# A two-layer attention and retention trunk on one core: three dense banks instead of two, logits and probabilities in one buffer, rows turned and outputs stored in one transfer

## The chip, the cores and the metric

The kernel runs on one core of one Trainium2 chip. The metric is the device time of one execution, in microseconds. A core has five engines with instruction streams of their own: PE (TensorE: matmuls, with weight loads shown apart as PEld), DVE (VectorE), ACT (ScalarE), POOL (GpSimd) and SP (SyncE, which here issues every DMA). They meet by semaphores only.

## The reference, cut

```
for layer in range(2):
    h    = rms_norm(x, norm_gain[layer])                     # x: 2048 x 1024, f32
    proj = h @ w_in[layer]                                   # 1024 x 4096, in 8 sections of 512:
    aq, ak, av, ag, rq, rk, rv, rg = split(proj)             # attention q,k,v,gate; retention q,k,v,gate
    # attention: 8 heads x 64; a query sees its own 64-token chunk and the 8 chunks before it
    s    = aq @ ak.T * 64**-0.5 + rel_bias[head, clip(distance)]
    ya   = softmax(s) @ av
    # retention: 4 heads x 128; rotary q and k, decay per head, running state, rms norm of each head's output
    yr   = rms_norm(decayed(rq, rk) @ rv + rq @ state)
    y    = concat[ya * silu(ag), yr * silu(rg)]
    x    = x + y @ w_out[layer]                              # 1024 x 1024
out = rms_norm(x, final_gain)
```

## The kernel before

**Precision.** Every large product is done as three f16 products of high and low parts (high x high, low x high, high x low): a matrix is kept as a pair of f16 tiles, whose sum carries the f32 value. So the products of 1024 inputs take 3 x 8 = 24 matmuls for one result bank.

**Tiling.** The 2048 tokens are four blocks n of 512, each of four tiles a of 128. The input projection of a layer goes by section s = 0 to 3: two attention heads and one retention head with all their parts. For each (layer, s, n) there are two dense generators. `dense_T` makes q, k, rotary q and rotary k (j = 0 to 3) transposed, channels on partitions and the block's 512 tokens as columns, with 24 matmuls of 128x512 each (L731; L712 for the very first block, which is done tile by tile). `dense_V` makes v, retention v and both gates, one token tile at a time (L752). Both need the block's normed input transposed, `hTh` and `hTl` (high and low). Their results lie in PSUM banks of the pool `psD`, two of them; ACT and DVE read a bank out, ending with L770 for the gate tile `gt`, before the bank is used again.

**Attention** runs one block behind, as 8 units (a, hx) of one token tile and one head. A unit: PE makes the logits S (L800, L801); DVE adds the bias and takes the row maximum (L804, out: f32 buffer `sc`); DVE turns the maximum into the exponential's bias, m * nc + LN_PSC (L806); ACT takes the exponential with scale g.c (L807) and copies it to f16 (L809, buffer `pq`); POOL subtracts for the low part (L810, same `pq`); SP transposes `pq` into `pT` by DMA (L812); two units later PE multiplies with v into a bank of `psR` (L820 to L822, tile `o`, whose column 64 holds the sum of the row), and DVE divides and applies the gate (`out_`, L826 to L832), then SP stores y (L835). `sc` and `pq` have two buffers each.

**Retention** (`decayed`, `retention`) makes r1, the decayed scores of a tile, r2, its output with the carried state, and a new state; DVE makes the f16 low parts (`rest_of`, L868), POOL the power for the norm (L921), DVE applies norm and gate (L925) and SP stores its half of y.

**Rows.** Where normed rows are made on ACT and DVE, they are a pair of f16 rows, one in a buffer of `sc` and one in a buffer of `pq` (`row_pair`), and `transpose_rows` turns both with one DMA transpose each (L236, L237). That happens for the norms of the first layer's blocks 2 and 3 (during s = 0), for some norms between the layers, and for each tile's y ahead of the output projection (`y_squares` L958, `rows_hi`, `rows_lo`, `y_turn`).

**Output projection** (`wout`): 16 tiles of 48 matmuls (L1105), in six rounds a tile. `wout_first` prepares the first two y rows. The last attention units of a layer run beside its first tiles.

**Order.** The programs of PE, ACT, DVE and POOL are in the order in which the Python code emits them. Generators are advanced in rounds: `run` steps a dense generator and the attention generator together, `later(k, fn)` puts a step k rounds on, `push` queues background work (weights, norms, tables) and `pull` takes steps of it. SP's order is left to a scheduler after the first section. A wait of one instruction holds all that follow on its engine.

**The start.** Weights, the gains, rotary tables (`tables`, stored to DRAM and loaded by block) and the norms of the first eight tiles are made in the first 80 us, in an order written by hand.

Of the kernel before, what the change touches and what calls it, by code (L numbers as in the profile page):

```python
# [27 lines left out]
def hybrid_trunk(ctx: ExitStack, tc: tile.TileContext, x, pos, gain, gcol, w_in, w_out, rel, fgain,  # L28
# [33 lines left out]
    pool.memset(mhalf, -0.5)  # L62
    invf_sb = cp.tile([P, 1], F32, tag="invf", name="invf_sb")
# [6 lines left out]
    tab_d = [dp.tile([2, P, 512], F32, tag=f"tab{n}", name=f"tab{n}") for n in range(NS)]  # L70
# [12 lines left out]
    def tables(n, wk):  # L83

        ang, k, r, k2 = wk
# [40 lines left out]
        for hf in range(2):  # L126
            sl = slice(hf * 64, hf * 64 + 64)
            cs = slice(hf * 256, hf * 256 + 256)
            sp.dma_start(tab_d[n][0, 0:64, cs], k2[sl, :])
            sp.dma_start(tab_d[n][0, 64:128, cs], k2[sl, :])  # L130
            sp.dma_start(tab_d[n][1, 0:64, cs], ang[sl, :])
            sp.dma_start(tab_d[n][1, 64:128, cs], r[sl, :])
# [82 lines left out]
    def hT_of(l, n):  # L215
        if (l, n) not in hT:
            hT[l, n] = (hp.tile([P, KT, 512], F16, tag="hTh", name=f"hTh{l}_{n}"),
                        hp.tile([P, KT, 512], F16, tag="hTl", name=f"hTl{l}_{n}"))
        return hT[l, n]

    def row_pair(nm):
        return (b2.tile([P, 1280], F16, tag="sc", name=f"rh{nm}")[:, 0:D],
                b2.tile([P, 1280], F16, tag="pq", name=f"rl{nm}")[:, 0:D])
# [11 lines left out]
    def transpose_rows(rows, dh, dl):  # L235
        sp.dma_start_transpose(out=dh, in_=rows[0])  # L236
        sp.dma_start_transpose(out=dl, in_=rows[1])  # L237

    class Tok:


        def __init__(self, t, xt, rows):
            self.t, self.x, self.rows, self.nm = t, xt, rows, f"n0_{t}"
            self.hh, self.hl = (h_[:, :, t % 4 * P:(t % 4 + 1) * P] for h_ in hT_of(0, t // 4))
# [21 lines left out]
        def hi(self):  # L266
            if self.rows:
                self.rw = (self.rows[:, 0:D], self.rows[:, D:2 * D])
                act.activation(self.rw[0], self.x, AF.Copy)
                return  # L270
            for h in range(2):
                act.activation(self.hh[:, h * KT // 2:(h + 1) * KT // 2, :], self.pt[h], AF.Copy)

        def lo(self):
            if self.rows:
                dve.tensor_tensor(self.rw[1], self.x, self.rw[0], op=ALU.subtract)
                return
# [4 lines left out]
        def dma(self):  # L282
            transpose_rows(self.rw, self.hh, self.hl)
# [324 lines left out]
    def dense_T(l, s, n, g, st):  # L608
        hh, hl = hT[l, n]
        nm = f"{l}_{s}_{n}"  # L610
        st.tabc = b1.tile([P, 512], F32, tag="tabc", name=f"tabc{nm}")
        st.tabs = b1.tile([P, 512], F32, tag="tabs", name=f"tabs{nm}")
        def tab_load():
            while n not in tab_done:
                pull(1)
            sp.dma_start(st.tabc, tab_d[n][0])
            sp.dma_start(st.tabs, tab_d[n][1])
# [9 lines left out]
        def evacuate(j, ps):  # L627
            if j == 0:
                st.q = b2.tile([P, 2, 2, 512], F16, tag="q", name=f"q{nm}")
                qq = b1.tile([P, 2, 512], F16, tag="qq", name=f"qq{nm}")  # L630
# [10 lines left out]
            elif j == 1:  # L641
                st.k = b3.tile([P, 2, 512], F16, tag="k", name=f"k{nm}")
                kk = b1.tile([P, 2, 512], F16, tag="swp", name=f"kk{nm}")
                kh, kl = kk[:, 0, :], kk[:, 1, :]
                act.activation(kh, ps, AF.Copy, scale=2.0 ** -16)

                def k_rest():
                    dve.scalar_tensor_tensor(out=kl, in0=ps, scalar=2.0 ** -16, in1=kh, op0=ALU.mult, op1=ALU.subtract)
                    sp.dma_start(st.k[0:64, 0, :], kh[0:64, :])
                    sp.dma_start(st.k[64:128, 1, :], kh[64:128, :])  # L650
                    sp.dma_start(st.k[64:128, 0, :], kl[0:64, :])
                    sp.dma_start(st.k[0:64, 1, :], kl[64:128, :])

                soon(k_rest)
            else:
                w = 5 - j
                rot = b2.tile([P, w, 512], F16, tag=f"rot{j}", name=f"rot{nm}_{j}")
                if j == 2:
                    raw = rot[:, 1:3].rearrange("p a c -> p (a c)").bitcast(F32)
                else:  # L660
                    raw = b1.tile([P, 512], F32, tag="qq", name=f"raw{nm}")
                act.activation(raw, ps, AF.Copy, scale=2.0 ** -16)

                def swap(rot=rot, raw=raw, j=j):
                    swp = b1.tile([P, 512], F32, tag="swp", name=f"swp{nm}_{j}")
# [20 lines left out]
                    later(d, turned(raw, raw, st.tabc, ALU.mult))  # L686
                    later(d + 1, turned(swp, swp, st.tabs, ALU.mult))
# [30 lines left out]
        for j in range(2 if first else 0, 4):  # L718
# [19 lines left out]
    def dense_V(l, s, n, g, st):  # L738
        hh, hl = hT[l, n]
# [38 lines left out]
    def attention(l, s, n, g, st, prev, nxt):  # L778
# [4 lines left out]
        ya = {}  # L783

        def qk(a, hx):
# [10 lines left out]
            for j0, j1 in zip(cuts, cuts[1:]):  # L796
# [5 lines left out]
            v = b2.tile([P, 640], F32, tag="sc", name=f"sc{u.nm}")[:, 0:w]  # L802
            m = b2.tile([P, 1], F32, tag="mq", name=f"mq{u.nm}")
            dve.tensor_tensor_reduce(out=v, in0=S[:, 0:w], in1=g.bias[hx][:, 640 - w:640], scale=1.0, scalar=-3.0e38,  # L804
                                     op0=ALU.add, op1=ALU.max, accum_out=m)
            dve.tensor_scalar(m, m, g.nc[:, 0:1], LN_PSC, op0=ALU.mult, op1=ALU.add)  # L806
            act.activation(v, v, AF.Exp, bias=m[:, 0:1], scale=g.c[:, 0:1])  # L807
            pq = b2.tile([P, 1280], F16, tag="pq", name=f"pq{u.nm}")
# [6 lines left out]
        def pv(u):  # L815
            t = 4 * n + u.a
            o = psR.tile([P, 512], F32, tag="small", name=f"o{u.nm}")
            for b, (q_, a_) in enumerate(u.kts):
# [3 lines left out]
                pe.matmul(o[:, 0:65], u.p[:, u.nb + b, :], v_[:, 0:65], start=False, stop=(b == u.nb - 1))  # L822

            def out_():
# [14 lines left out]
        ret = retention(l, s, n, g, st)  # L839
# [30 lines left out]
    def decayed(l, s, n, g, st, a):  # L870
        nm = f"{l}_{s}_{4 * n + a}"
        cs = slice(a * P, (a + 1) * P)
        r1 = psR.tile([P, 512], F32, tag="small", name=f"r1{nm}")
        products(r1[:, 0:P], [(st.rk[:, i, cs], st.rq[:, j, cs]) for i, j in ((0, 0), (0, 1), (1, 0))])

        def upper():
            st.dT = b1.tile([P, 2, P], F16, tag="dT", name=f"dT{nm}")
            upper_of(st.dT, r1[:, P:2 * P])

        later(1, lambda: dve.tensor_tensor(r1[:, P:2 * P], r1[:, 0:P], g.msk, op=ALU.mult))  # L880
        later(2, upper)
        later(3, lambda: rest_of(st.dT, r1[:, P:2 * P]))

    def retention(l, s, n, g, st):
        for a in range(4):
# [5 lines left out]
            r2 = psR.tile([P, 512], F32, tag="small", name=f"r2{nm}")  # L891
# [6 lines left out]
            if not last:  # L898
# [16 lines left out]
                later(3, lambda sh=sh, ns=ns: rest_of(sh, ns))  # L915
# [7 lines left out]
            def fin(t=t, a=a, r2=r2, ss=ss, nm=nm):  # L923
                y = b1.tile([P, P], F32, tag="yr", name=f"yr{nm}")
# [591 lines left out]
```

## Time and profile before

| | before |
|---|---|
| median of 3 runs (lowest to highest), us | 2094.98 (2092.48 to 2095.95) |
| profiled execution, us | 2094.75 |
| its span, us | 2092.8 |
| mean granted TensorE clock | 0.991 |
| PE / DVE / ACT / POOL busy, us | 2004.4 / 1343.8 / 1141.3 / 432.9 |
| matmuls | 14014 |
| DMA, mean over the span | 150 GB/s |

The span runs from the first to the last instruction of the profiled execution. A row of the timeline has the start in us, the duration, the engine, the line, the operation with out<-in, and in square brackets the idle time of the engine before it with what ended it. A row of the view of waits has the total in us, the number of times and the longest. A row of busy time by stage has PE, PEld, DVE, ACT and POOL with their counts, then the granted clock, the share of DMA and GB/s. A 512-column matmul is shown as 0.38 us long, but the next starts 0.216 us after it, as matmuls overlap.

### The profile page before, as it was taken

What the parts mean: (1) busy time and instruction counts of PE and PEld (TensorE: products, weight loads), DVE (VectorE), ACT (ScalarE), POOL (GpSimd) and SP (SyncE); (2) the same over time, 40 slices, a digit from 0 to 9 for tenths busy, and PEclk for the clock granted to TensorE, in tenths of its full rate; (3) what the DMA queues carried; (4) which work ended last, traced back from release to release, by engine and by line L of the source; (5) the groups of instructions that cost most, each with busy time, mean ns of one, the idle gap of its engine ahead of it and who ended that gap; (6) DMA issues with size and microseconds to landing.
All of it is one profiled execution on the core that took longest, in us unless ns stands there. A gap on an engine that the chain in (4) does not pass through costs nothing.

```text
span 2092.8 us, 39599 instructions
## 1 busy us (share of the span) xinstructions
PE 2004.4 (96%) x14014; PEld 1049.4 (50%) x14014; DVE 1343.8 (64%) x4031; ACT 1141.3 (55%) x2522; POOL 432.9 (21%) x509
## 2 busy tenths in 40 slices
PE   6888999999999999998999999999999999998998
PEld 4344455555555555444444555555555555554443
DVE  7676666666656666576654666666666667656643
ACT  7455665556565654455444546554655565455432
POOL 1022222222122212121000222222222222222100
PEclk9999999999999999999999999999999999999999
DMA  8767674557476764599965556655655776558874
GB/s 247 171 127 162 136 166 114 115 112 159 110 169 133 161 166 99 113 211 260 219 185 113 120 102 142 130 121 106 155 123 118 178 156 162 117 100 183 212 199 123
DMA packets 645702, 313.65 MB, mean 150 GB/s; under 512 B 459232, under 2 KB 602080, under 8 KB 645504
## 3 DMA queue, kind: packets, MB, share of 16 engines
q1 hardware_dynamic: 645504, 311.12, 66.4%
q8 instruction: 110, 1.80, 0.4%
q14 instruction: 88, 0.72, 0.1%
HBM read 123.26 MB, written 41.98 MB: 79 GB/s over the span
## 4 chain that ended last, share of the span: by engine, by line
PE 55%; DMA 7%; DVE 5%; ACT 3%; issue 1%; SPq 1%; POOL 0%; POOLq 0%; DVEq 0%; ACTq 0%
PE dT L731 18%; PE dV L752 15%; PE dO L1105 12%; DMA pT<-pq 2%; PE r L860 2%; PE S L801 2%; PE S L800 2%; PE o L820 1%; PE o L821 1%; PE o L822 1%; DVE sc L804 1%; DMA swp<-rot 1%; DMA yhy<-rhy 1%; ACT sc L807 1%; ACT pq L809 1%
## 5 line engine op out<-in xcount | busy, mean ns | idle before, releaser
L810 POOL TENSOR_TENSOR pq<-sc,pq 128x640 f16<-128x640 f32 (+4 forms) x256 | 323.8, 1265 | 1175.9 <-issue 590.7
L807 ACT ACTIVATE sc<-sc,mq,cT 128x640 f32<-128x640 f32 (+4 forms) x256 | 218.5, 853 | 558.1 <-DVE mq L806 413.7
L752 PE MATMUL dV<-whV,hTh 128*128 128x512 f16 x1024 | 354.5, 382 | 13.0 <-DVE gt L770 12.8
L731 PE MATMUL dT<-hTh,whT 128*128 128x512 f16 x1008 | 349.4, 382 | 14.7 <-DMA hTh<-hTl 9.6
L752 PE MATMUL dV<-wlV,hTh 128*128 128x512 f16 x1024 | 354.1, 381 | 0.0
L752 PE MATMUL dV<-whV,hTl 128*128 128x512 f16 x1024 | 354.0, 381 | 0.0
L731 PE MATMUL dT<-hTl,whT 128*128 128x512 f16 x1008 | 346.6, 379 | 0.0
L731 PE MATMUL dT<-hTh,wlT 128*128 128x512 f16 x1008 | 346.6, 379 | 0.0
L752 PEld LDWEIGHTS <-hTh 128*128 128x128 f16 x2048 | 197.3, 98 | 227.7 <-DVE gt L770 16.4
L731 PEld LDWEIGHTS <-whT 128*128 128x128 f16 x2016 | 192.9, 98 | 221.6 <-issue 24.1
L804 DVE CUSTOM_DVE_ANT_0 sc<-S,bias 128x640 f32<-128x640 f32 (+4 forms) x256 | 188.4, 736 | 78.8 <-PE S L801 61.1
L1105 PE MATMUL dO<-whO,yly 128*128 128x512 f16 x512 | 194.1, 379 | 2.4 <-DMA yly<-rly 2.4
L1105 PE MATMUL dO<-whO,yhy 128*128 128x512 f16 x512 | 194.0, 379 | 1.2 <-DVE gt L770 0.6
L1105 PE MATMUL dO<-wlO,yhy 128*128 128x512 f16 x512 | 194.0, 379 | 0.0
L809 ACT ACTIVATE pq<-sc 128x640 f16<-128x640 f32 (+4 forms) x256 | 171.5, 670 | 10.9 <-DMA pT<-pq 3.0
L1105 PEld LDWEIGHTS <-yhy 128*128 128x128 f16 x1024 | 99.6, 98 | 115.1 <-issue 0.8
L752 PEld LDWEIGHTS <-hTl 128*128 128x128 f16 x1024 | 99.7, 98 | 105.0 <-issue 2.8
L800 PE MATMUL S<-k,q 128*128 128x128 f16 (+3 forms) x592 | 143.1, 268 | 7.9 <-DVE mq L804 7.9
L731 PEld LDWEIGHTS <-wlT 128*128 128x128 f16 x1008 | 97.2, 98 | 101.8 <-issue 1.1
L820 PE MATMUL o<-v,pT 128*128 128x65 f16 x1120 | 129.6, 193 | 10.2 <-DMA pT<-pq 9.7
L801 PE MATMUL S<-k,q 128*128 128x128 f16 (+3 forms) x592 | 130.5, 268 | 0.0
L820 PEld LDWEIGHTS <-pT 128*128 128x128 f16 x1120 | 105.3, 97 | 49.2 <-DMA pT<-pq 21.3
(350 smaller groups left out, 3352.7 us busy)
## 6 DMA issues: line engine op xcount, KB each, us to landing
q<-qq SPq DMA_DIRECT2D x128, 128.0 KB, 2.7
yyy<-y_d SPq DMA_DIRECT2D x32, 512.0 KB, 4.6
stT<-in_w_in_dram SPq DMA_DIRECT2D x27, 512.0 KB, 4.8
stV<-in_w_in_dram SPq DMA_DIRECT2D x26, 512.0 KB, 4.5
k<-kk SPq DMA_DIRECT2D x128, 64.0 KB, 2.0
swp<-rot SPq DMA_DIRECT2D x64, 128.0 KB, 2.5
tabc<-tab SPq DMA_DIRECT2D x32, 256.0 KB, 2.7
tabs<-tab SPq DMA_DIRECT2D x32, 256.0 KB, 2.9
```

What stands on the lines that cost most here:

```text
L731: pe.matmul(ps, w_[:, j, kt, :], h_[:, kt, :], start=(m == 0), stop=(m == 23))
L752: pe.matmul(ps, h_[:, kt, a * P:(a + 1) * P], w_[:, kt, :], start=(m == 0), stop=(m == 23))
L800: pe.matmul(o, st.q[:, hx, 0, cs], k_, start=True, stop=False)
L801: pe.matmul(o, st.q[:, hx, 1, cs], k_, start=False, stop=True)
L804: dve.tensor_tensor_reduce(out=v, in0=S[:, 0:w], in1=g.bias[hx][:, 640 - w:640], scale=1.0, scalar=-3.0e38, op0=ALU.add, op1=ALU.max, accu ...
L807: act.activation(v, v, AF.Exp, bias=m[:, 0:1], scale=g.c[:, 0:1])
L809: act.activation(pq[:, 0:w], v, AF.Copy)
L810: pool.tensor_tensor(pq[:, w:2 * w], v, pq[:, 0:w], op=ALU.subtract)
L820: pe.matmul(o[:, 0:65], u.p[:, b, :], v_[:, 0:65], start=(b == 0), stop=False)
L821: pe.matmul(o[:, 0:64], u.p[:, b, :], v_[:, 65:129], start=False, stop=False)
L860: pe.matmul(out_, w_, m_, start=(i == 0), stop=(i + 1 == len(pairs)))
L1105: pe.matmul(ps, h_[:, kt, :], w_[:, kt, :], start=(m == 0), stop=(m == 23))
```

## The change

- `psD` gets three banks, `psR` three instead of four. Both heads' o of a tile lie in one bank and are divided out together, with one reciprocal of two columns; r1 and r2 of a tile share a bank.
- In the first section of layer 0, blocks 1 to 3, q and k are done in four parts of 128 columns (one per token tile), tile by tile, q and k in turn: 144 matmuls of 512 columns become 576 of 128.
- `hTh` and `hTl` are one tile, and so are a pair of rows: one DMA transpose of 16 blocks takes the place of two of 8.
- The f32 logits and the f16 pair are two halves of one buffer, `spq`, with two buffers in all; row pairs use the same two.
- DVE's reduction multiplies by nc and takes the minimum; the added constant is put on by POOL in a 128x1 addition, and ACT's exponential has scale -1.
- The gate tile takes y in place, and one DMA stores both halves, when attention and retention of the tile are both done. The rotary tables are stored with four DMAs a block instead of eight and loaded with one instead of two.
- `rest_of` of the state comes a round later (4 instead of 3). `wout_first` is pushed behind `prep_O(l, 1)` at the last block of the last section, not ahead of it.

```diff
-    psD = ctx.enter_context(tc.tile_pool(name="psD", bufs=2, space=PSUM))
+    psD = ctx.enter_context(tc.tile_pool(name="psD", bufs=3, space=PSUM))
     psS = ctx.enter_context(tc.tile_pool(name="psS", bufs=1, space=PSUM))
-    psR = ctx.enter_context(tc.tile_pool(name="psR", bufs=4, space=PSUM))
+    psR = ctx.enter_context(tc.tile_pool(name="psR", bufs=3, space=PSUM))
...
-        for hf in range(2):
-            sl = slice(hf * 64, hf * 64 + 64)
-            cs = slice(hf * 256, hf * 256 + 256)
-            sp.dma_start(tab_d[n][0, 0:64, cs], k2[sl, :])
-            sp.dma_start(tab_d[n][0, 64:128, cs], k2[sl, :])
-            sp.dma_start(tab_d[n][1, 0:64, cs], ang[sl, :])
-            sp.dma_start(tab_d[n][1, 64:128, cs], r[sl, :])
+        parts = wk[:, 0:768].rearrange("p (a c) -> p a c", c=256)
+        for h in range(2):
+            for hf in range(2):
+                sp.dma_start(tab_d[n][h * 64:h * 64 + 64, :, hf * 256:hf * 256 + 256],
+                             parts[hf * 64:hf * 64 + 64, h:3:2 - h])
...
     def row_pair(nm):
-        return (b2.tile([P, 1280], F16, tag="sc", name=f"rh{nm}")[:, 0:D],
-                b2.tile([P, 1280], F16, tag="pq", name=f"rl{nm}")[:, 0:D])
+        return halves_of(b2.tile([P, 2560], F16, tag="spq", name=f"rw{nm}")[:, 0:2 * D])
...
-    def transpose_rows(rows, dh, dl):
-        sp.dma_start_transpose(out=dh, in_=rows[0])
-        sp.dma_start_transpose(out=dl, in_=rows[1])
+    def transpose_rows(rows, dst):
+        sp.dma_start_transpose(out=dst, in_=rows[2])
...
+        second = (l, s) == (0, 0) and n > 0
+        if second:
+            ps = [psD.tile([P, 512], F32, tag="dense", name=f"dT{nm}_{j}") for j in range(2)]
+            m = 0
+            for (j, a) in ((j, a) for a in range(4) for j in range(2)):
+                while g.tdone <= j:
+                    pull(1)
+                cs = slice(a * P, (a + 1) * P)
+                for i, (w_, h_) in enumerate((w_, h_) for (w_, h_) in ((g.h, hh), (g.l, hh), (g.h, hl)) for kt in range(KT)):
+                    kt = i % KT
+                    pe.matmul(ps[j][:, cs], w_[:, j, kt, :], h_[:, kt, cs], start=(i == 0), stop=(i == 23))
+                    m += 1
+                    if m % 32 == 0 and m < 192:
+                        yield
+                if a == 3:
+                    evacuate(j, ps[j])
+            yield
-        for j in range(2 if first else 0, 4):
+        for j in range(2 if first or second else 0, 4):
...
-            v = b2.tile([P, 640], F32, tag="sc", name=f"sc{u.nm}")[:, 0:w]
+            spq = b2.tile([P, 2560], F16, tag="spq", name=f"spq{u.nm}")
+            v, pq = spq[:, 0:1280].bitcast(F32)[:, 0:w], spq[:, 1280:2560]
             m = b2.tile([P, 1], F32, tag="mq", name=f"mq{u.nm}")
-            dve.tensor_tensor_reduce(out=v, in0=S[:, 0:w], in1=g.bias[hx][:, 640 - w:640], scale=1.0, scalar=-3.0e38,
-                                     op0=ALU.add, op1=ALU.max, accum_out=m)
-            dve.tensor_scalar(m, m, g.nc[:, 0:1], LN_PSC, op0=ALU.mult, op1=ALU.add)
-            act.activation(v, v, AF.Exp, bias=m[:, 0:1], scale=g.c[:, 0:1])
-            pq = b2.tile([P, 1280], F16, tag="pq", name=f"pq{u.nm}")
+            dve.tensor_tensor_reduce(out=v, in0=S[:, 0:w], in1=g.bias[hx][:, 640 - w:640], scale=g.nc[:, 0:1],
+                                     scalar=3.0e38, op0=ALU.add, op1=ALU.min, accum_out=m)
+            pool.tensor_tensor(m, m, lnp, op=ALU.add)
+            act.activation(v, v, AF.Exp, bias=m[:, 0:1], scale=-1.0)
...
             def out_():
-                rl = b2.tile([P, 1], F32, tag="rl", name=f"rl{u.nm}")
-                dve.reciprocal(rl, o[:, 64:65])
-                dve.tensor_tensor(rl, rl, g.ka, op=ALU.mult)
-                if u.hx == 0:
-                    ya[u.a] = b2.tile([P, P], F32, tag="ya", name=f"ya{u.nm}")
-                y = ya[u.a]
-                vs = slice(u.hx * 64, u.hx * 64 + 64)
-                dve.scalar_tensor_tensor(out=y[:, vs], in0=o[:, 0:64], scalar=rl[:, 0:1], in1=st.g[u.a][:, vs],
-                                         op0=ALU.mult, op1=ALU.mult)
-                if u.hx == 1:
-                    sp.dma_start(y_d[t][:, s * P:(s + 1) * P], y)
+                rl = b2.tile([P, 2], F32, tag="rl", name=f"rl{u.nm}")
+                dve.reciprocal(rl, o2[:, 0:2, 64])
+                dve.tensor_scalar(rl, rl, g.ka[:, 0:1], None, op0=ALU.mult)
+                for hx in range(2):
+                    y = st.g[u.a][:, hx * 64:hx * 64 + 64]
+                    dve.scalar_tensor_tensor(out=y, in0=o2[:, hx, 0:64], scalar=rl[:, hx:hx + 1], in1=y, op0=ALU.mult,
+                                             op1=ALU.mult)
+                finished(u.a)
...
-                later(3, lambda sh=sh, ns=ns: rest_of(sh, ns))
+                later(4, lambda sh=sh, ns=ns: rest_of(sh, ns))
...
-                if n == NS - 1 and s == NSW - 1:
-                    us = []
-                    push(wout_first(l, go, us), 10)
...
                         push(prep_O(l, 1, gO[1], go), 9)
+                        us = []
+                        push(wout_first(l, go, us), 10)
```

More of the change, by code (lines that the diff above doesn't have):

```diff
@@ L69, in hybrid_trunk @@
     x_d = [dp.tile([P, D], F32, tag=f"x_d{t}", name=f"x_d{t}") for t in range(NT)]
-    tab_d = [dp.tile([2, P, 512], F32, tag=f"tab{n}", name=f"tab{n}") for n in range(NS)]
+    tab_d = [dp.tile([P, 2, 512], F32, tag=f"tab{n}", name=f"tab{n}") for n in range(NS)]
     TWO_PI = 6.283185307179586
@@ L83, in tables @@
     def tables(n, wk):
-        ang, k, r, k2 = wk
+        ang, r, k2, k = (wk[:, i * 256:(i + 1) * 256] for i in range(4))
         pi = k2.bitcast(I32)
@@ L274, in lo @@
         def lo(self):
-            if self.rows:
+            if self.rows is not None:
                 dve.tensor_tensor(self.rw[1], self.x, self.rw[0], op=ALU.subtract)
@@ L999, in mul @@
         def mul():
-            u.x = xt if on_pe or rows else psS.tile([P, D], F32, tag="S", name=f"xn{nm}")
+            u.x = xt if on_pe or rows is not None else psS.tile([P, D], F32, tag="S", name=f"xn{nm}")
             dve.scalar_tensor_tensor(out=u.x, in0=xt, scalar=u.rs[:, 0:1], in1=gains[l].b, op0=ALU.mult, op1=ALU.mult)
@@ L1011, in upper @@
             else:
-                u.rows = rows or row_pair(nm)
+                u.rows = halves_of(rows) if rows is not None else row_pair(nm)
                 rows_hi(u.rows, u.x)
@@ L1273, in hybrid_trunk @@
     sp.dma_start(invf_sb, invf)
-    t0 = tables(0, [gp.tile([P, 256], F32, tag="gt", name=f"wk{i}") for i in range(4)])
+    t0 = tables(0, b2.tile([P, 2560], F16, tag="spq", name="wk").bitcast(F32)[:, 0:1024])
     go_on(t0)
```

126 lines of the change are left out of this document (73 added, 53 removed).

## The prediction

> **What bounds the kernel now.** I read the page first, then its busy time by stage, then PE's waits, then the timeline at each long pause.
>
> The page (busy us and share; the 40 slices of the span):
>
> ```profile
> span 2092.8 us, 39599 instructions
> PE 2004.4 (96%) x14014; PEld 1049.4 (50%) x14014; DVE 1343.8 (64%) x4031; ACT 1141.3 (55%) x2522; POOL 432.9 (21%) x509
> PE   6888999999999999998999999999999999998998
> DMA  8767674557476764599965556655655776558874
> ```
>
> PE is the bound and nearly full, except in slices 0 to 3, around 18 and around 36. Busy time by stage says the same in us:
>
> ```profile
> 50.00:100.00 50.00, 40.16 (x199) 18.42 (x197) 32.59 (x81) 24.55 (x50) 4.32 (x11) 0.90 0.72 164
> 100.00:210.00 110.00, 91.10 (x614) 46.41 (x612) 79.15 (x219) 61.19 (x131) 25.38 (x29) 0.94 0.73 148
> 350.00:870.00 520.00, 516.23 (x3857) 275.85 (x3856) 340.03 (x1077) 294.99 (x689) 126.17 (x139) 1.00 0.63 133
> 870.00:970.00 100.00, 88.83 (x627) 45.28 (x626) 67.00 (x184) 55.54 (x105) 22.28 (x22) 0.97 0.94 209
> 1090.00:1870.00 780.00, 776.06 (x5636) 411.04 (x5635) 503.42 (x1573) 435.00 (x1025) 180.36 (x204) 1.00 0.60 131
> 1870.00:1970.00 100.00, 93.33 (x695) 49.40 (x694) 69.49 (x201) 56.32 (x112) 24.17 (x25) 0.98 0.80 181
> ```
>
> From 350 to 870 PE is idle 3.8 us of 520, and from 1090 to 1870 3.9 of 780: a shorter DVE or SP program is worth nothing there. There is something to win between 50 and 210 us (28.7 us idle, at a granted clock of 0.90 and 0.94: layer 0, first section) and in the two stretches where the last attention units run beside the output projection (11.2 and 6.7 us idle). What PE waits for, over the span:
>
> ```profile
> PE dV L752 <- DVE gt L770: 12.8, 6, 4.9
> PE o L820 <- DMA pT<-pq: 9.7, 11, 2.2
> PE dT L731 <- DMA hTh<-hTl: 9.6, 1, 9.6
> PE S L800 <- DVE mq L804: 7.9, 4, 3.3
> PE dT L731 <- DMA hTh<-rhn: 2.8, 1, 2.8
> PE dT L731 <- issue: 2.2, 1, 2.2
> PEld L820 <- DMA pT<-pq: 21.3, 25, 2.7
> ```
>
> The long ones in PE's timeline (start, us, operation, idle before):
>
> ```profile
> 68.89 0.38 PE L752 MATMUL dV<-wlV,hTh 128*128 128x512 f16 x1
> 78.91 1.01 PE L731 MATMUL dT<-hTh,whT 128*128 128x512 f16 x2 [9.64 <-DMA hTh<-hTl]
> 129.54 0.61 PE L752 MATMUL dV<-whV,hTh 128*128 128x512 f16 x1 [4.88 <-DVE gt L770]
> 192.54 0.61 PE L752 MATMUL dV<-whV,hTh 128*128 128x512 f16 x1 [4.25 <-DVE gt L770]
> 204.90 3.40 PE L731 MATMUL dT<-hTh,whT 128*128 128x512 f16 x8 [2.81 <-DMA hTh<-rhn]
> 862.23 1.89 PE L752 MATMUL dV<-whV,hTl 128*128 128x512 f16 x8
> 878.17 0.27 PE L800 MATMUL S<-k,q 128*128 128x128 f16 x1 [3.28 <-DVE mq L804]
> 1891.00 0.27 PE L800 MATMUL S<-k,q 128*128 128x128 f16 x1 [3.18 <-DVE mq L804]
> ```
>
> A pause costs more than itself: after 2.81 us of idle, eight matmuls took 3.40 us, where eight take 1.89 us at 862: 1.5 us more. The Trainium skill ("TensorE: Matmul & The Clock Gate", Part 1) says that the clock falls to half after an idle window of some 3.4 us; here a shorter pause was followed by it too. I put 1.5 us on each of the six long pauses above.
>
> **The change, part by part.** Against the profiled execution's own time, 2094.75 us (span 2092.8), which lies 0.2 us under the median of the three timed runs, 2094.98.
>
> *Column parts for q and k in blocks 1 to 3 of the first section.* Before, the 512-column matmul at 78.91 needs the transposes of all four tiles 4 to 7. On SP's queue:
>
> ```profile
> 49.17 0.60 SPq L129 DMA_DIRECT2D tab<-wk  x1
> ...
> 53.64 0.59 SPq L132 DMA_DIRECT2D tab<-wk  x1
> ...
> 58.77 1.47 SPq L237 DMA_TRANSPOSE hTl<-hTh  x1
> ...
> 74.73 2.92 SPq L237 DMA_TRANSPOSE hTl<-hTl  x1
> ```
>
> The eight table stores run from 49.17 to 54.2. The first tile's pair of transposes is issued by 60.2; the last pair's second half starts at 74.73 and PE starts at 78.91. With parts, tile 4 can be used when PE comes free at 69.1, and each part has 2 x 24 matmuls of 128 columns, some 2.7 us, so PE would come to tile 7 at about 77. Four of the eight table stores (0.6 us each) and one of the two transposes of each tile (1.5 and 2.9 in these rows) leave SP's queue ahead of it, so the last tile should land some us before 78.9 rather than at it. I take 1.5 us as left over: -9.6 -1.5 +1.5 = **-9.6** (bounds -11.1 and -6, where the last tile still lands at 78.9 and PE waits again, and at low clock).
>
> The same parts, and rows that are turned in one transpose, act on the waits of blocks 2 and 3, 2.2 (issue) and 2.81 + 1.5: at most -6.5. They were short because PE came late to them: PE will now be some 10 to 20 us ahead, and the norms that feed them need not be. **-4** (0 to -6.5).
>
> The price of the parts: 144 matmuls become 576.
>
> ```profile
> 906.40 0.33 PE L860 MATMUL r<-rot,rot 128*128 128x128 f16 x3
> 906.57 0.38 PE L1105 MATMUL dO<-wlO,yhy 128*128 128x512 f16 x1
> ```
>
> Three 128-column matmuls, each with a weight load, move PE on by 0.17 us: 57 ns each (55 to 58 by rounding). Four are 228 ns, and one of 512 is 1.89 less a pipeline tail: with the tail of 0.38 - 0.216 the eight take 0.216 each. So 144 x 12 ns = 1.7 us, 0.6 at the lower rounding: **+1**. The Trainium skill ("TensorE: Matmul & The Clock Gate", Part 2, "Back-to-back issue gap") gives about 81 ns per 128-column matmul in a sustained stream with weight loads; by it the parts would cost 144 x (324 - 216) = 15.6 us. Our row is a burst of three, the parts run 32 in a row, so this stays as a rival.
>
> *Third bank for dense results.* The waits on gt L770 are waits for one of two banks: with three, the tile that needs the bank comes one tile (24 x 0.216 = 5.2 us) later. That covers 4.88 and 4.25, with 1.5 us of low clock each, -12.1; of the other 3.7 us in that row one or two lie in this section. **-13** (-6, if ACT, which writes v and rv ahead of gt, stays late for two tiles running, to -15.8). The bank comes from psR, 4 to 3; both heads' o share one bank, r1 and r2 one, so fewer are asked for; a gap there would delay o or r. Nothing in the trace shows a wait for these banks, so 0 (to +5, one wait of 0.5 in each of ten blocks).
>
> *Output projection pushed five rounds later; 878 and 1891.* PE waits there for the DVE reduction, and of that operation the view grouped by shape says:
>
> ```profile
> L804 DVE CUSTOM_DVE_ANT_0 sc<-S,bias 128x640 f32<-128x640 f32 x192 | 157.3, 819 | 69.1 <-PE S L801 51.6 <-DMA yhy<-rhy 10.1 <-PE msV L323 5.9
> ```
>
> Twice, for 10.1 us together, it waits for the transposes of y rows 0 and 1, which took both row buffers back to back. In the new order units lie between those rows, so these two pauses should go: 3.28 + 3.18 + 2 x 1.5 = 9.5 at most; what is late next is the y row itself, which starts later: **-7** (0 to -9.5).
>
> *Scale in the minimum, add on POOL.* In each unit the DVE operation between reduction and exponential goes, and a one-column POOL operation comes:
>
> ```profile
> L921 POOL TENSOR_TENSOR rss<-rss,mhalf 128x1 f32<-128x1 f32 x128 | 72.5, 567 | 139.1 <-DVE rss L920 130.6 <-ACT rv L762 7.2 <-DVE m2T L325 1.3
> L806 DVE TENSOR_SCALAR mq<-mq,ncT 128x1 f32<-128x1 f32 x256 | 54.8, 214 | 9.1
> ```
>
> 0.567 for 0.214, and one more handover between engines: some 0.5 us later per unit. It is hidden where the transposed pT lands well before its use; it is not in the 11 + 25 cases above where PE or its weight loads wait for pT. 36 x 0.5 = 18 at most; for the 11 in which the matmul itself is released last, **+5** (0 to +18). On POOL the previous unit's subtraction and the powers of the retention's norm stand in line with the add; POOL is 21% busy, so that is rarely more. DVE gets 55 us and half of the reciprocals back, off the path.
>
> *Logits and probabilities in one buffer.* Before, a unit's reduction needed only the f32 buffer, free after POOL's subtraction; now it needs the whole buffer, free when pT of the unit two allocations back has landed. In the full stretches that is long past. It is not where rows take every third buffer: the output projection with units, and norms in the first section.
>
> ```profile
> 906.52 0.81 DVE L804 CUSTOM_DVE_ANT_0 sc<-S,bias 128x640 f32<-128x640 f32 x1
> 910.93 1.34 SPq L812 DMA_TRANSPOSE pT<-pq  x1
> DMA to landing us min/median/max: 3.4/4.7/5.1
> 904.12 1.04 ACT L958 ACTIVATE rhy<-yyy 128x1024 f16<-128x1024 f32 x1
> 914.79 1.75 SPq L237 DMA_TRANSPOSE yly<-rly  x1
> 949.37 1.06 ACT L958 ACTIVATE rhy<-yyy 128x1024 f16<-128x1024 f32 x1 [3.16 <-DMA yhy<-rhy]
> ```
>
> A unit holds a buffer from 906.52 to 910.93 + 4.7 = 915.6, 9.1 us and 9.6 with the POOL add; a y row from 904.12 to 914.79 + some 4, 14.7, less 1.7 for the transpose saved: 13. Three cycles of one row and two units take 949.37 - 904.12 = 45.3, 15.1 each, in which two buffers give 30.2 us; 2 x 9.6 + 13 = 32.2 are asked for, 1 us too much per cycle. The order (unit, row, unit) makes a row wait for the whole unit before it, and a row wait is there already (3.16). So 1 to 2.8 us on each of five cycles in each of two layers, while queued behind the waiting reduction on DVE are the evacuations of the output and the norms: **+12** (0 to +28). In the first section four units meet norm rows in the same way, each late by one landing, 3.4, at most: **+4** (0 to 14).
>
> *At nothing:* one store of y for two and one table load for two shorten SP's queue, which is not last in the full stretches; that store now waits for the later of its two halves, and what SP has queued behind it waits too, which the full stretches cover; the state's rest a round later stands under PE work of a whole round. If that cover is gone each costs a us.
>
> Sum: -9.6 -4 +1 -13 -7 +5 +12 +4 = -11.6, so 2094.75 - 11.6 = **2083**.
>
> **The rivals.**
> - *Slower: the shared buffer sets the pace beside the output projection.* For it: the row above already waits 3.16 us for a buffer, and DMA is busy 0.94 there. Against: the row's hold is partly waiting for its own round, which may shrink. Its price is +28 and +14: 2094.75 - 9.6 - 4 + 1 - 13 - 7 + 5 + 28 + 14 = 2109. It decides the sign from about 2.4 us per cycle (11.6 more than my 12, over ten cycles). Chance 0.24.
> - *The start is bound by transfers, not by the order of work.* Then both waits on hT stay (DMA share is 0.72 there): the sum without -9.6 and -4 is +2.0, 2097. Against: transposes and stores are themselves cut. 0.13.
> - *Nothing is given back:* every pause named goes, and only half of the pT price is met: -11.1 -6.5 -15.8 -9.5 +1 +5 = -37, 2058. 0.13.
> - *128-column matmuls with weight loads are slower in long bursts than in threes.* If loads, busy 1049.4 us for 14014 (75 ns each with overlaps), can't be hidden behind 57 ns, a part costs some 25 ns more per matmul: 576 x 25 = 14 us, 2097. 0.03. The Trainium skill's 81 ns (the section above) is this case.
>
> **How the numbers follow.** My forecast has 0.47 and a range of its own of 2072 to 2095. A measurement of this kernel can tell about 0.2%, 4.2 us, from no change. Faster by more: 0.41 of the forecast, 0.13 and 0.02 of the second rival: 0.56. Within: 0.05, 0.08 of the second and 0.01 of the last: 0.14. Slower: 0.24, 0.03, 0.02 and 0.01 of the forecast: 0.30. The range from 2058 to 2108 leaves out half of the first and of the third rival.
>
> **What would show it.** Right: no pause of 9 us near 70 to 79; no wait of dV on gt over 1 us before 210; PE busy over 105 of 110 in what was 100 to 210; full stretches unchanged to 1 us; the reduction waiting for pT's transposes in the ten output cycles, with tokens of the output projection 1 to 2 us further apart. Wrong: the stretches from 350 to 870 or 1090 to 1870 longer by over 3 us (the POOL add or the smaller psR would have reached the path), or waits on hT as long as before.

## The result: 2384.6 us, 14% slower

The changed kernel takes 2384.61 us (median of 4, 2375.75 to 2386.39) against 2093.84 for the kernel before (median of 4, 2092.48 to 2095.95): a ratio of 1.1379, 95% interval 1.1348 to 1.1410. I had forecast 2083. No case that I priced came near it: the highest was 2109.

The profile after, page (as shown of before):

```profile
span 2374.0 us, 39669 instructions
...
PE 2077.2 (87%) x14446; PEld 1100.1 (46%) x14446; DVE 1239.7 (52%) x3519; ACT 1120.9 (47%) x2522; POOL 524.4 (22%) x766
...
PE   6877779997989799878999997999799888996898
...
PEclk9999889998999899989999998999899999998999
```

The span grew by 281 us. PE's busy time grew by 73 (2077.2 for 2004.4) and its idle time by 208 (296.8 for 88.4). The holes are no longer in a few slices but all over, and the granted clock has dips to 8 where it had none. The stages that had been full tell it best (us, then PE, PEld, DVE, ACT, POOL busy, clock, DMA share, GB/s):

```profile
350.00:870.00 520.00, 464.37 (x3280) 244.64 (x3278) 264.99 (x824) 254.57 (x608) 131.37 (x194) 0.94 0.54 120
1090.00:1870.00 780.00, 715.59 (x4701) 367.47 (x4700) 412.75 (x1176) 380.38 (x868) 161.01 (x241) 0.96 0.58 133
1240.00:2140.00 900.00, 813.75 (x5731) 427.67 (x5729) 459.37 (x1355) 433.63 (x1039) 220.80 (x325) 0.96 0.53 114
```

Idle 55.6 of 520 and 64.4 of 780 us, where it had been 3.8 and 3.9, at a clock of 0.94 and 0.96 for 1.00. The same times are not quite the same work: by 1090 the changed kernel is still in the first layer's output projection (its tiles begin at 1027 to 1223 us). The third row has the sections of the second layer alone, idle 86.3 of 900. And PE's waits have a new first row:

```profile
PE r L889 <- DVE r L910: 248.1, 67, 9.5
PE msT L327 <- DVE mbT L320: 6.3, 2, 3.4
```

The waits that the prediction had listed are nearly gone: none on gt, none on hT for the column parts, none of S for the reduction. That alone does not show that the third bank or the parts took them away, since PE now comes late to everything: in the first experiment below, with two dense banks and the order of before, the waits on gt, on pT and of S are gone as well. One wait has taken the place of all. PE's timeline in the second section (start, us, idle before in brackets), and DVE's at that place:

```profile
394.64 0.33 PE L889 MATMUL r<-rot,rot 128*128 128x128 f16 x3
...
400.69 0.27 PE L889 MATMUL r<-rv,dT 128*128 128x128 f16 x2 [3.36 <-DVE r L910]
...
402.49 0.63 PE L773 MATMUL dV<-wlV,hT 128*128 128x512 f16 x1
```

```profile
384.15 0.29 DVE L910 TENSOR_TENSOR r<-r,msk 128x128 f32<-128x128 f32 x1
...
399.74 0.68 DVE L674 TENSOR_TENSOR tmp<-tmp 128x512 f32<-128x512 f32 x1
400.35 0.29 DVE L910 TENSOR_TENSOR r<-r,msk 128x128 f32<-128x128 f32 x1
400.55 0.28 DVE L787 SCALAR_TENSOR_TENSOR v<-dV,v 128x128 f16<-128x128 f32 x1
```

At 394.64 PE makes r1 of tile a+1 (rot times rot). One round later it wants to make r2 of tile a (rv times dT), and stands still until DVE has masked r1 of tile a+1 at L910. The two have nothing to do with each other, except the bank. `decayed` for tile a+1 runs a round ahead of `retention` for tile a and has by then set `ring["rr"]` to its own bank, so `ring.pop("rr")` gives r2 not the bank of its own tile's r1, masked at 384.15, but that of the next tile's r1, which DVE has yet to mask. The program makes PE's first matmul into that bank wait for DVE's write in the same bank, although r2 lies in other columns of it than r1. The mask stands in DVE's line behind whatever came first, here among others thirteen one-column operations (397.01 to 399.83) and a rotary multiply. ACT's dT of the next tile in turn waits for PE (100.6 us in 47 places over the span).

After the pause the matmul at 402.49 takes 0.63 us for 0.38: the low clock adds to the wait. The granted clock (last but two in the row) fell to a half 1.3 us after PE had resumed:

```profile
402.03:405.44 3.41, 3.41 (x17) 1.55 (x16) 0.86 (x3) 0.00 (x0) 0.00 (x0) 0.50 0.35 92
```

The Trainium skill ("TensorE: Matmul & The Clock Gate", Part 1) puts the fall to half clock at an idle window of some 3.4 us. The pause of 3.36 us is about that long, but of the 3.41 us ahead of the fall PE was idle only 2.07 (398.62 to 400.69), and the pause of 2.81 us in the prediction was followed by slow matmuls too: here less than a whole idle window was enough.

### The profile page after: what moved, and what is told of

It reads as the page before. It is cut to its first block, busy times and chain, and to the rows that moved or that the text cites. A ratio compares the mean times of both kernels' runs of the same rounds, so it can differ in the third digit from the quotient of the medians.

```text
span 2374.0 us, 39669 instructions
## 1 busy us (share of the span) xinstructions
PE 2077.2 (87%) x14446; PEld 1100.1 (46%) x14446; DVE 1239.7 (52%) x3519; ACT 1120.9 (47%) x2522; POOL 524.4 (22%) x766
## 5 line engine op out<-in xcount | busy, mean ns | idle before, releaser
L773 PE MATMUL dV<-whV,hT 128*128 128x512 f16 x2048 | 617.2, 396 | 0.0
L836 ACT ACTIVATE spq<-spq,mq 128x640 f32<-128x640 f32 (+4 forms) x256 | 194.9, 761 | 810.4 <-POOL mq L835 805.6
L752 PE MATMUL dT<-hT,whT 128*128 128x512 f16 x1920 | 556.5, 383 | 0.0
L773 PEld LDWEIGHTS <-hT 128*128 128x128 f16 x3072 | 299.7, 101 | 332.4 <-issue 36.6
L838 POOL TENSOR_TENSOR spq<-spq 128x640 f16<-128x640 f32 (+4 forms) x256 | 324.0, 1266 | 415.3 <-issue 357.3
L773 PE MATMUL dV<-wlV,hT 128*128 128x512 f16 x1024 | 356.0, 383 | 0.0
L833 DVE CUSTOM_DVE_ANT_0 spq<-S,bias,ncT 128x640 f32<-128x640 f32 (+4 forms) x256 | 204.0, 797 | 263.7 <-PE S L829 205.7
L752 PE MATMUL dT<-hT,wlT 128*128 128x512 f16 x960 | 336.0, 383 | 0.0
L1138 PE MATMUL dO<-whO,yTy 128*128 128x512 f16 x960 | 296.2, 387 | 3.9 <-DMA yTy<-rwy 3.8
L889 PE MATMUL r<-rv,dT 128*128 128x128 f16 x384 | 67.7, 237 | 254.4 <-DVE r L910 248.1
L752 PEld LDWEIGHTS <-whT 128*128 128x128 f16 x1920 | 184.8, 99 | 196.9 <-issue 10.3
L1138 PE MATMUL dO<-wlO,yTy 128*128 128x512 f16 x480 | 186.4, 388 | 0.0
L752 PEld LDWEIGHTS <-wlT 128*128 128x128 f16 x960 | 93.6, 99 | 99.4 <-issue 4.7
```

The source lines that it names most:

```text
L752: pe.matmul(ps, w_[:, j, kt, :], h_[:, kt, :], start=(m == 0), stop=(m == 23))
L773: pe.matmul(ps, h_[:, kt, a * P:(a + 1) * P], w_[:, kt, :], start=(m == 0), stop=(m == 23))
L836: act.activation(v, v, AF.Exp, bias=m[:, 0:1], scale=-1.0)
L838: pool.tensor_tensor(pq[:, w:2 * w], v, pq[:, 0:w], op=ALU.subtract)
L1138: pe.matmul(ps, h_[:, kt, :], w_[:, kt, :], start=(m == 0), stop=(m == 23))
```

## The experiments

Twelve kernels. First: is it the shared bank, by itself?

**One part alone, in the kernel before.** r1 moves to the last quarter of its bank and r2 pops that bank; everything else stays.

```diff
-        r1 = psR.tile([P, 512], F32, tag="small", name=f"r1{nm}")
+        ring["rr"] = psR.tile([P, 512], F32, tag="small", name=f"r1{nm}")
+        r1 = ring["rr"][:, 3 * P:4 * P]
...
-            r2 = psR.tile([P, 512], F32, tag="small", name=f"r2{nm}")
+            r2 = ring.pop("rr", None)
+            if r2 is None:
+                r2 = psR.tile([P, 512], F32, tag="small", name=f"r2{nm}")
```

> The kernel before with one part of the change alone: r2 of a tile takes the bank that r1 got last (which is r1 of the next tile), mask done in place; psD 2 and psR 4 stay. Theory A (shared bank: PE's first matmul of r2 must wait until DVE has masked the next tile's r1, which stands in DVE's line one round later): 2300 to 2400 us, with PE waiting some 200 us or more for the mask. Theory B (the mask is late only because the changed logit chain and POOL add have put DVE's and ACT's order out): 2095 to 2130. Theory C (it is the fourth psR bank that is missing): 2090 to 2100.

2313.84 us, one run (executions of one kernel differ by up to 11 us here), against 2097.16: +217. PE's waits in it:

```profile
PE r L860 <- DVE r L881: 199.3, 68, 12.4
PE dT L731 <- DMA hTh<-hTl: 9.1, 1, 9.1
```

Theory A, and neither B nor C: here the logit chain is the old one and psR has four banks.

**The same part undone, in the changed kernel** (psR has to go back to four banks for it, psD to two).

```diff
-            r2 = ring.pop("rr", None)
-            if r2 is None:
-                r2 = psR.tile([P, 512], F32, tag="small", name=f"r2{nm}")
+            r2 = psR.tile([P, 512], F32, tag="small", name=f"r2{nm}")
```

> The changed kernel with r2 in a bank of its own again, for which psR goes back to four banks and psD to two; all other parts of the change stay. Theory A: the wait for the mask goes, and what is left is the sum of the prediction without the third bank, 2094.75 + 1.4: 2075 to 2105 us. Theory B: DVE stays late for other readers, over 2200. Theory C: like A, 2075 to 2105.

2168.59 us, ratio 1.0338 (1.0319 to 1.0356): 216 us less than the changed kernel, nearly the same amount from the other side, though here a bank has moved from psD to psR as well. The wait is gone. But 2168.6 is not the 2075 to 2105 that I expected: 71 us of loss are left. Its PE waits:

```profile
PE r L889 <- DVE sh L897: 26.6, 18, 5.8
PE dT L732 <- DVE gt L791: 22.6, 3, 9.1
PE o L850 <- DMA pT<-spq: 17.4, 20, 2.0
PE dV L773 <- DVE gt L791: 10.5, 6, 2.7
```

**Mask one round earlier**, bank still shared: `dve.tensor_tensor(r1, r1, g.msk, ...)` at once and not in `later(1, ...)`.

> The changed kernel, bank still shared, psD 3 and psR 3, but DVE's mask of r1 is issued in the round of r1 itself, one round earlier in DVE's line. Theory A: the mask is done a round sooner, the wait of r2 shrinks to a part: 2090 to 2200 us, PE's wait for the mask under 100. Theory B: DVE is late by itself, 2300 or more. Theory C: nothing changes, 2370 to 2390.

2312.43 us, one run: 72 less, the wait on the mask 163.2 us in 51 places for 248.1 in 67. The direction is A's, but 2312 lies in B's range of 2300 or more, and the wait is not under 100. One round is not enough: on average the mask starts 2.5 us after the end of r1, for 3.0 in the changed kernel (worked out from the two traces), since other work stands ahead of it in DVE's line; only in seven places does DVE itself wait for r1, 5.1 us in all.

**r2 in its own tile's bank**: `next(ret)` ahead of `decayed(a + 1)`, psR 4, psD 2.

> The changed kernel with r2 of a tile emitted ahead of r1 of the next tile, so that r2 takes the bank of its own tile's r1, masked four rounds before; psR 4 and psD 2 as the bank lives longer. Theory A: no wait for the mask at r2, 2075 to 2110 us; what may be late instead is the chain r1, mask, dT, which has one round less: at most some us per tile. Theory B: over 2200. Theory C: 2075 to 2110.

2186.12 us, one run. No wait for the mask, with r1 and r2 still in one bank: it is the wrong tile's bank that costs, not the sharing as such. It is 18 more than with a bank of its own, and outside what I gave. The wait of o for pT is 23.5 us there for 17.4, and retention's for dT 5.0.

So some 216 of the 291 us come from the bank of the wrong tile. What is left was taken apart next, against the run with r2 in its own bank (2168.59).

**Logits and probabilities in two buffers again.**

```diff
-            spq = b2.tile([P, 2560], F16, tag="spq", name=f"spq{u.nm}")
-            v, pq = spq[:, 0:1280].bitcast(F32)[:, 0:w], spq[:, 1280:2560]
+            v = b2.tile([P, 1280], F16, tag="sc", name=f"sc{u.nm}").bitcast(F32)[:, 0:w]
...
+            pq = b2.tile([P, 1280], F16, tag="pq", name=f"pq{u.nm}")
             act.activation(pq[:, 0:w], v, AF.Copy)
```

> The run with r2 in its own bank (psR 4, psD 2; 2168.6 us), and logits and probabilities again in two buffers of two each, as before, row pairs in one of each with two transposes. (The rotary table's scratch at the start, which lay in the shared buffer, lies in the table's own tile.) Theory A (the shared buffer sets the pace where rows take every third buffer: it cost 11 and 16 us in the two output stretches and a part of the first section): 2135 to 2150 us, with the output tokens 1 to 4 back at 13 to 15 us. Theory B (what is left of the loss is the column parts holding both dense banks): 2160 to 2170. Theory C (it is the state's rest a round later): 2160 to 2170.

2134.23 us, ratio 1.0188 (1.0172 to 1.0203): 34 less. (The single transpose of a pair of rows is undone with it, so what that may have saved is taken off.) With the shared buffer DVE's reduction waits for pT; without it no such row is left, only 1.6 us for y rows. ACT's square of a y row waits as well. Both rows are of the run with the shared buffer:

```profile
DVE spq L833 <- DMA pT<-spq: 34.4, 19, 3.2
```

```profile
923.46 1.06 ACT L987 ACTIVATE rwy<-yyy 128x1024 f16<-128x1024 f32 x1 [3.51 <-DMA pT<-spq]
```

The time from one output tile's first matmul to the next one's (worked out from PE's records, us; before, shared buffer, two buffers):

```
layer 0, tile 0    15.00   14.93   15.05
         tile 1    13.05   15.59   13.05
         tile 2    13.04   16.17   13.04
         tile 3    14.76   18.02   14.10
         tile 4    13.79   18.52   16.81
layer 1, tile 0    14.02   14.97   16.77
         tile 1    13.13   18.81   13.67
         tile 2    13.04   15.35   13.04
         tile 3    12.78   20.41   13.00
```

These nine tiles take 24 us less with two buffers. Not all are back: tile 4 of layer 0 and tile 0 of layer 1 stay 3 us longer than before.

**No column parts** (`second = False`).

> The run with r2 in its own bank (psR 4, psD 2; 2168.6 us) without the column parts: q and k of blocks 1 to 3 of the first section in 512 columns again. Theory B (with two dense banks the parts hold both over the whole of q and k, and each bank's evacuation stops PE): the first section gets 15 to 22 us shorter, 2145 to 2155 us, though the wait of 9 us near 70 comes back. Theory A and C: within 5 us of 2168, as the parts cost nothing but their 1 us.

2152.92 us, ratio 1.0273 (1.0256 to 1.0291): 16 less, as theory B has it. With two banks the parts' q and k hold both at once, and the part that begins a block waits for the block before's last gate: the row of 22.6 us on dT L732 above is gone; 4.7 us of waits for hT are back.

**The state's rest three rounds on** (`later(3, ...)` for `later(4, ...)`).

> The run with r2 in its own bank (psR 4, psD 2; 2168.6 us) with the low half of the state made three rounds on again, not four. Theory C (r2 waits for the state's low half: 26.6 us in 18 waits in that run, against 2.4 in 3 before): 2135 to 2150 us. Theories A and B: 2160 to 2170, as those waits only stand in for others.

2164.06 us, ratio 1.0329 (1.0314 to 1.0345): 4.5 less, with intervals that overlap, so not clear of noise. The wait on sh left the list, but gt on dV went from 10.5 to 14.9 us and the output's wait for a y row to 13.3: those 26.6 us mostly stood in for others. Theory C falls.

**Third dense bank with r2 in its own bank**: psD 3, psR 3, the small sums over partitions in psD.

> The changed kernel (psD 3, psR 3) with r2 in a bank of its own; the banks of the small sums over partitions come from psD, so that psR's three are one each for o, r1 and r2. Theory A and B: the third dense bank takes away what the parts cost with two, so 2140 to 2160 us, the shared buffer's 27 us staying. Rival D (three psR banks are too few: r2 of a tile has to wait until the tile before has been normed): PE waits at r2 or o on DVE, 2180 to 2300.

2192.63 us, ratio 1.0471 (1.0451 to 1.0491): 24 more than with psD 2 and psR 4. Rival D:

```profile
PE o L850 <- DVE gt L862: 53.3, 25, 4.1
PE r L889 <- DVE gt L955: 27.6, 12, 6.7
...
PE dT L752 <- DVE gt L791: 1.0, 1, 1.0
```

The waits on gt L791 are down to 1.0 us (with two banks 22.6 and 10.5, and 6.6 at dT L752), as I said of the third bank; but three psR banks cost more than that, and while PE stands 81 us for them, what the third bank is worth by itself cannot be read from this run. It does give the price of the sharing with three banks in each pool: 2384.6 - 2192.6 = 192 us, and 24 for the exchange of banks, together the 216 (the small sums moved pools, too).

**y in tiles of its own.**

```diff
-                    y = st.g[u.a][:, hx * 64:hx * 64 + 64]
-                    dve.scalar_tensor_tensor(out=y, in0=o2[:, hx, 0:64], scalar=rl[:, hx:hx + 1], in1=y, op0=ALU.mult,
-                                             op1=ALU.mult)
-                finished(u.a)
+                    vs = slice(hx * 64, hx * 64 + 64)
+                    dve.scalar_tensor_tensor(out=ya[:, vs], in0=o2[:, hx, 0:64], scalar=rl[:, hx:hx + 1],
+                                             in1=st.g[u.a][:, vs], op0=ALU.mult, op1=ALU.mult)
+                t = 4 * n + u.a
+                sp.dma_start(y_d[t][:, s * P:(s + 1) * P], ya)
```

> The run with r2 in its own bank (psR 4, psD 2; 2168.6 us), and y again written to tiles of its own and stored with one DMA for each half, so that the gate's buffer is free when y has been made, not when its store has landed. Theory E (in that run ACT waits 38.7 us in 23 places for the store before it may write a gate, which holds a dense bank, which holds PE: 33 us of waits on gt L791): 2145 to 2158 us, with ACT's wait for the store gone and PE's waits on gt under 20 us. Rival (banks alone decide, the gate's buffer is hidden): 2164 to 2170.

2149.10 us, ratio 1.0244 (1.0229 to 1.0258): 19.5 less. The row that had led to it is ACT's, in the run with r2 in its own bank:

```profile
ACT gt L782 <- DMA y_d<-gt: 38.7, 23, 4.4
```

In place, y keeps the gate's buffer until its store has landed; ACT waits for that before it can write the next gate, and holds a dense bank while it waits. With tiles of its own that row is gone, and PE's wait of the parts on gt falls from 22.6 to 12.3 us. With 10.6 at dV that makes 22.9, not under 20 as expected.

**All five undone together**, and then **the constant on DVE too**.

> The changed kernel with five parts undone together: r2 in its own bank (psR 4, psD 2), logits and probabilities in two buffers each, no column parts, the state's rest three rounds on, y in tiles of its own. There stay: both heads' o in one bank and divided out together, the minimum with the POOL add, one tile for the high and low halves of the turned input, tables stored and loaded in fewer DMAs, the output projection's start five rounds later. If the single costs add up: 2168.6 - 34 - 16 - 4.5 - 15 = 2099 us. Theory F (the POOL add is a cost of its own, ACT's wait for it being 600 us): 2100 to 2115, with PE waits for pT over 10 us. Rival (what stays is gain): 2080 to 2090.

> The kernel of the run before, with the constant added by DVE and not by POOL (same sum, the minimum stays). Theory F (the handover to POOL and back costs about 0.5 us per unit, and shows where pT is late): 4 to 15 us less than with POOL. Rival (the add is hidden, as units two apart give it time): within 3 us of it.

2094.18 us, ratio 0.9982 (0.9972 to 0.9991), and 2078.56 us, ratio 0.9906 (0.9893 to 0.9919). The first lies between the two ranges given, 2100 to 2115 and 2080 to 2090. The single costs add up: 2168.59 - 34.4 - 15.7 - 4.5 - 19.5 = 2094.5. That it fits to 0.3 us is luck: the runs were made on different chips, and by each ratio to the runs of before beside it the four are 31, 14, 2 and 20, 67 in sum for 75 measured. The POOL add costs 15.6 us, a little over the 4 to 15 expected. ACT's wait in front of the exponential, with the add on POOL and then on DVE, each followed by PE's waits in the same run:

```profile
ACT sc L840 <- POOL mq L839: 605.4, 255, 5.8
```

```profile
PE dV L778 <- DVE gt L796: 14.2, 11, 4.9
PE o L855 <- DMA pT<-pq: 11.4, 15, 2.1
PE dO L1144 <- DMA yTy<-rhy: 8.3, 4, 4.1
```

```profile
ACT sc L840 <- DVE mq L839: 425.3, 200, 4.8
ACT sc L840 <- DVE rl L863: 98.4, 40, 3.3
```

```profile
PE dV L778 <- DVE gt L796: 10.5, 8, 4.7
PE o L855 <- DMA pT<-pq: 8.1, 9, 2.0
PE dO L1144 <- DMA yTy<-rhy: 5.8, 4, 2.2
```

With the add on DVE, ACT waits there for other rows of DVE too, so all of them have to be counted: 556.5 us for 605.4 with POOL, 0.2 us for each of the 256 units. The add itself has a median of 0.19 us on POOL and 0.16 on DVE, so most of that is the handover. Three waits of PE fall by 3.7, 3.3 and 2.5 us: the gate stands behind the exponential in ACT's line, and comes late with it. These are 9.5 of the 15.6 us; where the rest went, these rows do not show. The Trainium skill ("GPSIMD Engine Reference", 4.1) names VectorE, not GpSimd, for an elementwise add on a tile; the runs agree for one column too (15.6 us). The last kernel beats both: what is left of the change (both heads divided out together, the minimum, one turned tile for both halves, fewer table DMAs, the output's start later, and parts of the diff that the list of changes does not name, such as the scratch tiles of q and k laid in one) is worth 18 us against 2096.5. It was not taken apart. Its page:

```profile
span 2077.6 us, 39245 instructions
...
PE 2005.7 (97%) x14014; PEld 1051.6 (51%) x14014; DVE 1312.6 (63%) x3775; ACT 1118.7 (54%) x2522; POOL 435.6 (21%) x510
```

**Column parts alone, block 1 only, in the kernel before** (`second = (l, s, n) == (0, 0, 1)`).

> The kernel before, with the column parts alone and in block 1 of the first section only, where PE waited 9.6 us for the last tile's transposes; two dense banks, everything else as before. If the parts do there what the prediction said: 2084 to 2091 us, the wait near 70 under 3 us. Rival (the parts hold both dense banks, and the matmuls behind them wait instead, as in the runs with two banks): 2092 to 2100.

2099.68 us, ratio 1.0010 (0.9998 to 1.0021): nothing, as the rival has it. PE does not wait for tiles 4 to 7 any more; it waits longer for a bank:

```profile
82.21 1.04 PE L728 MATMUL dT<-hTh,whT 128*128 128x128 f16 x8 [11.34 <-DVE gt L787]
```

```profile
78.76 0.69 DVE L670 TENSOR_TENSOR raw<-raw,tabc 128x512 f32<-128x512 f32 x1 [7.55 <-DMA swp<-raw]
...
81.74 0.41 DVE L787 SCALAR_TENSOR_TENSOR gt<-gt,dV 128x256 f32<-128x256 f32 x1
```

DVE stands 7.55 us in front of a rotary multiply until a swap's DMA has landed, and the evacuation of the last gate, which frees the second bank, stands behind it. The parts take q and k in turn and so need that bank after 24 short matmuls. In the kernel before, DVE stood there as long, under PE's wait for hT and the 24 long matmuls of q:

```profile
78.11 0.69 DVE L670 TENSOR_TENSOR raw<-raw,tabc 128x512 f32<-128x512 f32 x1 [7.20 <-DMA swp<-raw]
```

The rival of 81 ns per 128-column matmul is settled by the changed kernel's trace. There 531 of the 562 matmuls that directly follow another one of the parts start 55 or 56 ns after it, and 30 start 106 or 107 ns after it, at the half clock; each has a weight load of its own. Sixteen in a row:

```profile
85.24 1.06 PE L732 MATMUL dT<-hT,whT 128*128 128x128 f16 x16
```

So 576 of them take 32.3 us, where 144 of 512 columns took 31.1: the parts' matmuls cost 1.2 us.

## Why the prediction was wrong, step by step

- **The step that failed: "so fewer are asked for; ... Nothing in the trace shows a wait for these banks, so 0 (to +5 ...)".** It took r1 and r2 of one tile to share a bank, and asked only whether a bank would be free. It did not ask which tile's r1 is in the ring when r2 is emitted, nor what PE waits for when it writes a bank that DVE still works in. It measured +217 alone and -216 undone; with r2 in its own bank, three psR banks for four, put at 0 to +5 in the same step, cost 24 more, net of what the third dense bank gives. It could have been read from the code: the generator emits r1 of the next tile, then a round, then r2.
- **Column parts, -9.6 and -4.** The wait for hT did go, in the changed kernel. But its cover was not free time: with two banks the parts cost 15.7 us, and alone they gave nothing, since a bank held by DVE's order was late next. The +1 for the 432 extra matmuls was right, as the parts run at 56 ns a matmul, and the rival of 81 ns falls. (That rival's 25 ns more per matmul is not what the rows beside it give, 75 - 57 = 18.)
- **Third bank, -13.** The waits did go: where psD is 3 those on gt L791 are at most 1.0 us. The 13 us are not shown, as PE waited for other things in both of these kernels. The bank it was taken from costs more, +24 in sum with r2 in its own bank.
- **Output pushed later, -7.** The pauses of S on the reduction went, as said: 7.9 us before, 0.6 in the last kernel. With r2 in its own bank S waits 8.9 us on ACT in three places of the second layer's output (1990 to 2025 us); with logits and probabilities in two buffers that row is gone, so it comes with the shared buffer. The push was not tried alone.
- **POOL add, +5 (0 to +18).** 15.6: near the upper bound, and not by the sum that led there. The delay was put at 0.5 us per unit, from the duration of a power on POOL, where ACT's waits show 0.2; and I counted only the waits on pT, while ACT's line carries the gates and y rows behind the exponential too.
- **Shared buffer, +12 and +4 (0 to +28, 0 to +14).** 34.4: the mechanism was right, place and kind of wait as described; the size was double the value taken, within the sum of the bounds. The bound for one cycle was not: it was 2.8 us, and four of the tiles in the table above lose more, up to 7.4.
- **"At nothing".** The state's rest 4.5, within the error. y in the gate's buffer 19.5, missed: I looked at SP's queue behind the store, not at who waits for the buffer.
- **The rivals.** The shared buffer as the pace-setter came true in its place, but it is 34 of 291 us. None of the rivals named the bank. That of the start did not come true as it was put, since the wait for hT went; but another transfer, the swap's, was late next.

The sign that I had named for being wrong was there: the stretches from 350 to 870 and from 1090 to 1870 lost over 50 us of PE each, but neither of the two causes given with it, the POOL add and the smaller psR, was the main one: the sharing of a bank costs 217 us with four psR banks too. In measured sizes the change is -18 for what stays, +34 +16 +5 +20 +16 for the parts undone (2168.59 - 2078.56 = 90) and +216 for the bank: +288. This is a chain of differences from kernel to kernel, so it has to close; it does not test the parts. The changed kernel's own runs give 291, with another set of runs of before beside them.

## What to carry to other kernels

When two results share a bank or a buffer, write down the order in which the program emits their writers and readers, tile by tile: a ring that hands out "the last one" may hand out the next tile's. A buffer that lives longer (in place, merged, shared) is a new wait for whoever takes it next, and that engine's whole line waits with it. A wait that is removed has to be followed one step further: undo it alone and see what is late next.

## What the runs showed that I had not expected

The costs of the parts added up, within some 10 us, although they meet on the same engines; and the bank's share is nearly the same from both sides (+217 alone, -216 undone). And a wait of a few us at every other tile costs more than the wait: in the first experiment, which has the same 14014 matmuls as the kernel before, 199 us of waits for the mask came with 57 us more of busy time on PE (2061.3 for 2004.4), at a granted clock of 0.956 for 0.991.
